# Down projection in chunks of 6 block pairs with portions of a plain chunk between them, operand sets split at set steps, gate2 rows loaded by halves

## The chip, the cores and the metric

The kernel runs on one core of one Trainium2 chip. The metric is the device time of one execution in microseconds. Before the change the median of three runs is 2086.94 us (2086.75 to 2090.03).

## What is computed

One layer of a decoder trunk on 512 tokens of width 2048, everything in fp32. The change touches its last part, the ConvGLU with its residual, and the computing of one of the six modulation vectors, gate2:

```python
mod = (c_act @ ada_w[l] + ada_b[l])[:, None, :]
shift1, scale1, gate1, shift2, scale2, gate2 = jnp.split(mod, N_MOD, axis=-1)
...
h = rms_norm(x, ffn_norm_g[l]) * (1.0 + scale2) + shift2
x = x + gate2 * conv_glu(h, w_up[l], conv_w[l], conv_b[l], w_down[l])
...
def conv_glu(h, w_up, conv_w, conv_b, w_down):
    a, v = jnp.split(h @ w_up, 2, axis=-1)
    ...
    for tap in range(CONV_WIDTH):
        conv = conv + conv_w[tap] * ap[:, tap:tap + S]
    return (jax.nn.silu(conv) * v) @ w_down
```

w_up is 2048 x 11264 and w_down 5632 x 2048. What lies ahead (the first norm, the input projection, a gated recurrence, a pooling branch and the output projection) isn't touched.

## The kernel before

**Products.** Activations stand with their features on the 128 partitions and the 512 tokens in the free dimension. Every fp32 operand is split into a high part in the matmul's number format (a cast on ScalarE, `L120` for weights, `L176` for activations) and a low part (a subtraction on VectorE, `L121` and `L177`). A product takes three matmuls: high by high, high by low, low by high.

**Up projection.** The 5632 features of the GLU are 44 blocks j of 128; a group makes the two 128 x 512 results (gate and value) of one j. The first three are computed plainly. The other 41 go through a scheme that makes a 2 x 2 block product from seven products instead of eight: with the tokens cut into halves of 256 and the two outputs and two halves of the input features as blocks. So a group is seven steps, one for each product, in the order `SEQ`, P1, Q5, P2, P7, Q3, P6, Q4. Each step runs over 8 pairs of feature blocks: 24 matmuls of 256 columns (`product`, matmuls at `L816` to `L818`). The operands on the token side (sums and differences of the halves of h) are split once and held in SBUF for all groups. Behind each group come the GLU of the group before (`glu`: two ScalarE operations `L722`, `L725`, four of VectorE, `L723` among them) and `emit`, which writes the results to DRAM: for the pairs of blocks that go through the seven products below as seven operands of 128 x 256 (`od`), for the last four blocks as they are (`ad`).

**Down projection.** It sums over the 44 blocks. Twenty pairs of blocks go through the same seven products in three chunks of `SD` = 7, 7 and 6 pairs; each chunk has eight groups, one for each pair of output blocks f and f + 8, and a step runs over the chunk's 7 or 6 pairs (21 or 18 matmuls of 256 columns). Behind a group its two results, times gate2, are added to x1, the residual (`L1120`); the 16 tiles of x1 come back from DRAM (`x1d`, `L1093`), two ahead of each group of the first chunk. The last four blocks (`JD`) are a plain product over the 16 output blocks, in two halves of 256 tokens, with the final norm behind each half.

**Weights.** Class `Fast` plans the weights of all groups by step number, seven to a group. `load` asks SyncE's queue for four tiles of 128 x (128 x pairs) a group, `first` adds two of them (`L773`, VectorE), `dsum` adds a third in place by an accumulating DMA on GpSimd's queue (`L779`), `fourth` is another sum (`L783`), and `split` makes the high and low part of each product's weights one or two steps ahead. Raw weights, gate2 rows and (before) operands on their way share 9 buffers of 128 x 1024 (`rp`); split weights have 3 (`wp`); everything of 128 x 512 shares 73 (`tp`).

**Operand sets.** A chunk's seven operand sets replace those of the stage before. Each engine works in the program's order, and the order is this: in the last group of a stage, right behind the product that used an old set, `handover` drops that set and calls `operands`, which loads the new set of the same product from `od` in two pieces of 3 or 4 pairs into `rp` (`L1056`) and splits it at once, two pairs an operation (`L176`, `L177`; a single pair at `L1065`, `L1066`). So every set is loaded and split within one group.

**gate2.** Each of its 16 tiles is a row pair of two 128 x 1024 halves, multiplied by the activation of c and summed along the row on VectorE (`L102`). In the groups 7, 9 to 37 the two halves are asked for behind P1 and multiplied behind Q4 (`ada_load`, `ada_tile`).

## Time and profile before

| what | before |
|---|---|
| median of three runs (range) | 2086.94 us (2086.75 to 2090.03) |
| profiled execution, its own time | 2086.09 us |
| span of its profile | 2084.3 us |
| mean granted TensorE clock | 0.993 |
| TensorE busy | 2016.5 us, 97% |
| VectorE busy | 1731.1 us, 83% |
| ScalarE busy | 1021.5 us, 49% |
| moved by DMA | 451.6 MB, 217 GB/s in the mean |

The shares are means over the whole span. The program is a row of stages, and each is read for itself: the groups of the up projection lie between about 960 and 1600 us, the three down chunks between 1600 and 2021, the final plain block and the norm behind that. A stretch is judged by the number of its matmuls and the time that they take when nothing is late.

### The profile page before, as it was taken

What the parts mean: (1) busy time and instruction counts of PE and PEld (TensorE: products, weight loads), DVE (VectorE), ACT (ScalarE), POOL (GpSimd) and SP (SyncE); (2) the same over time, 40 slices, a digit from 0 to 9 for tenths busy, and PEclk for the clock granted to TensorE, in tenths of its full rate; (3) what the DMA queues carried; (4) which work ended last, traced back from release to release, by engine and by line L of the source; (5) the groups of instructions that cost most, each with busy time, mean ns of one, the idle gap of its engine ahead of it and who ended that gap; (6) DMA issues with size and microseconds to landing.
All of it is one profiled execution on the core that took longest, in us unless ns stands there. A gap on an engine that the chain in (4) does not pass through costs nothing.

```text
span 2084.3 us, 36447 instructions
## 1 busy us (share of the span) xinstructions
PE 2016.5 (97%) x14450; PEld 1867.4 (90%) x14450; DVE 1731.1 (83%) x2668; ACT 1021.5 (49%) x1527; POOL 135.7 (7%) x171
## 2 busy tenths in 40 slices
PE   7999999999999998999999999999999998998997
PEld 6888888888888888999999999999999998998997
DVE  8898899988877689888888888888888868778786
ACT  4323555565733365545445445444546435445455
POOL 0100000000000000000000000000000100100101
PEclk9999999999999999999999999999999999999999
DMA  9886877755586545788887787887878868768662
GB/s 371 321 287 223 272 235 244 248 177 184 192 294 226 172 168 121 192 247 228 218 217 213 213 215 211 215 221 203 222 223 248 224 174 254 188 165 222 163 173 81
DMA packets 163466, 451.60 MB, mean 217 GB/s; under 512 B 15552, under 2 KB 55776, under 8 KB 163296
## 3 DMA queue, kind: packets, MB, share of 16 engines
q1 hardware_dynamic: 144576, 385.31, 55.0%
q0 software_dynamic: 18720, 63.97, 18.1%
q8 instruction: 113, 1.85, 0.4%
q14 instruction: 57, 0.47, 0.1%
HBM read 421.41 MB, written 27.80 MB: 216 GB/s over the span
## 4 chain that ended last, share of the span: by engine, by line
PE 60%; DMA 14%; DVE 14%; issue 8%; ACT 3%; POOL 0%; SPq 0%; DVEq 0%; ACTq 0%; POOLq 0%
DMA raw<-in_dram 13%; PE mm L149 8%; PE mm L151 7%; PE mm L150 7%; PE mm L818 6%; PE mm L816 6%; PE mm L817 6%; DVE w L121 5%; PE sm L816 4%; PE sm L817 4%; PE sm L818 4%; ACT w L120 2%; DVE raw L102 2%; DVE raw L773 2%; DVE raw L783 1%
## 5 line engine op out<-in xcount | busy, mean ns | idle before, releaser
L120 ACT CAST w<-raw 128x1024 fp32r<-128x1024 f32 (+2 forms) x579 | 579.5, 1009 | 633.7 <-DVE raw L783 189.6
L121 DVE TENSOR_TENSOR w<-raw,w 128x1024 fp32r<-128x1024 f32 (+2 forms) x579 | 674.4, 1171 | 194.2 <-ACT w L120 193.7
L818 PE MATMUL mm<-hh,w 128*128 128x256 f32 x1952 | 545.8, 280 | 19.0 <-DVE w L121 18.4
L816 PE MATMUL mm<-hh,w 128*128 128x256 f32 x1952 | 542.5, 278 | 4.6 <-ACT w L120 4.5
L817 PE MATMUL mm<-hl,w 128*128 128x256 f32 x1888 | 523.6, 277 | 0.7 <-DVE hl L177 0.7
L816 PE MATMUL sm<-hh,w 128*128 128x256 f32 x1464 | 407.7, 278 | 5.4 <-ACT w L120 4.9
L818 PE MATMUL sm<-hh,w 128*128 128x256 f32 x1464 | 407.9, 279 | 2.9 <-DVE w L121 2.7
L817 PE MATMUL sm<-hl,w 128*128 128x256 f32 x1416 | 394.3, 278 | 4.7 <-DVE hl L177 4.7
L818 PEld LDWEIGHTS mm<-hh,w 128*128 128x128 f32 x1952 | 367.7, 188 | 26.9 <-DVE w L121 26.6
L816 PEld LDWEIGHTS mm<-hh,w 128*128 128x128 f32 x1952 | 367.8, 188 | 6.2 <-ACT w L120 5.3
L817 PEld LDWEIGHTS mm<-hl,w 128*128 128x128 f32 x1888 | 355.6, 188 | 1.2 <-DVE hl L177 1.1
L149 PE MATMUL mm<-hh,w 128*128 128x512 f32 x800 | 313.7, 401 | 14.8 <-ACT w L120 12.9
L151 PE MATMUL mm<-hh,w 128*128 128x512 f32 x800 | 313.8, 392 | 0.0
L150 PE MATMUL mm<-hl,w 128*128 128x512 f32 x800 | 313.1, 392 | 0.0
L102 DVE SCALAR_TENSOR_TENSOR raw<-raw,ca 128x1024 f32<-128x1024 f32 x192 | 232.4, 1222 | 74.6 <-DMA raw<-in_dram 73.8
L816 PEld LDWEIGHTS sm<-hh,w 128*128 128x128 f32 x1464 | 277.0, 189 | 6.5 <-ACT w L120 5.5
L818 PEld LDWEIGHTS sm<-hh,w 128*128 128x128 f32 x1464 | 277.0, 189 | 4.7 <-DVE w L121 4.5
L817 PEld LDWEIGHTS sm<-hl,w 128*128 128x128 f32 x1416 | 268.1, 189 | 5.4 <-DVE hl L177 5.4
L779 POOL DMA_DIRECT2D raw<-in_dram x130 | 112.6, 866 | 1455.6 <-DVE raw L773 904.8
L149 PEld LDWEIGHTS mm<-hh,w 128*128 128x128 f32 x800 | 151.3, 189 | 46.3 <-ACT w L120 12.9
L151 PEld LDWEIGHTS mm<-hh,w 128*128 128x128 f32 x800 | 151.2, 189 | 33.1 <-DVE w L121 0.8
L150 PEld LDWEIGHTS mm<-hl,w 128*128 128x128 f32 x800 | 151.5, 189 | 30.4 <-issue 0.5
(207 smaller groups left out, 2302.9 us busy)
## 6 DMA issues: line engine op xcount, KB each, us to landing
raw<-in_dram SPq DMA_DIRECT2D x532, 512.0 KB, 5.0
raw<-in_dram POOLq DMA_DIRECT2D x82, 512.0 KB, 5.9
raw<-in_dram SPq DMA_DIRECT2D x64, 448.0 KB, 4.5
od<-t SPq DMA_DIRECT2D x60, 256.0 KB, 3.5
raw<-in_dram POOLq DMA_DIRECT2D x32, 448.0 KB, 6.8
raw<-in_dram SPq DMA_DIRECT2D x32, 384.0 KB, 4.1
raw<-od SPq DMA_DIRECT2D x21, 512.0 KB, 4.9
t<-in_dram SPq DMA_DIRECT2D x32, 256.0 KB, 6.1
```

Source lines behind the costliest of these rows:

```text
L102: V.scalar_tensor_tensor(out=r, in0=r, scalar=1.0, in1=vec[i], op0=ALU.mult, op1=ALU.mult, accum_out=a[:, i:i + 1])
L120: A.copy(h, r)
L121: V.tensor_tensor(l, r, h.bitcast(F32), op=ALU.subtract)
L149: E.matmul(o, wH, mH, start=start, stop=False)
L150: E.matmul(o, wH, mL, start=False, stop=False)
L151: E.matmul(o, wL, mH, start=False, stop=stop)
L773: V.tensor_tensor(r, self.raw[n, P1], self.raw[n, "T"], op=ALU.add)
L779: G.dma_start(self.raw[n, key], self.groups[n][q], accum_op=ALU.add)
L783: V.tensor_tensor(t, t, self.raw.pop((n, P2)), op=ALU.add)
L816: E.matmul(o, wH[:, sl], mH, start=first and k == 0, stop=False, skip_group_check=True)
L817: E.matmul(o, wH[:, sl], mL, start=False, stop=False, skip_group_check=True)
L818: E.matmul(o, wL[:, sl], mH, start=False, stop=k == len(opnd) - 1, skip_group_check=True)
```

## The change

- **Chunks.** `SD` becomes 6, 6 and 6 pairs: 18 pairs instead of 20. The four blocks that come free form a second plain chunk of four blocks (`JD` = 4 and 4). Its product over 16 output blocks is cut into 8 portions of two output blocks (`middle`): one raw weight tile, loaded four steps ahead and split two steps ahead, 24 matmuls of 512 columns, and two updates of x1. `MID` puts three portions ahead of the first chunk, three ahead of the second and two ahead of the third. Step numbers of `Fast` are moved by one for each portion.
- **Operand sets.** `operands` falls into `oload` (three loads of 256 KB into tiles of the 73-tile pool) and `osplit`, which `Fast` calls at set steps. With F the first step of a chunk and M = F - m the first step of its portions, the sets are split in the order of `SEQ` at M - 4, M - 2, M, M + 1, M + 2, F + 1 and F + 3, and loaded two steps before. `release` only drops the old sets (and, behind the last chunk, prepares the final plain block).
- **x1.** Six tiles are asked for ahead of the first portions, the other ten two at a time by the groups of the first chunk, as far as the portions have not.
- **gate2.** One half row is loaded behind P2 and multiplied behind P6 in each of the groups 7 to 38.

```diff
 NCH = T // P
 NJ = 44
 NP0 = 3
-SD = (7, 7, 6)
-JD = (4,)
+SD = (6, 6, 6)
+MID = (3, 3, 2)
+JD = (4, 4)
...
@@ -103,8 +104,8 @@
                                    accum_out=a[:, i:i + 1])
...
@@ -737,13 +738,21 @@
     class Fast:


-        def __init__(self, groups):
+        def __init__(self, groups, extra):
             self.groups = groups
             self.events = {}
             self.hl, self.raw = {}, {}
             self.at = -100
+            self.start = []
+            u = 0
             for n in range(len(groups)):
-                s = 7 * n
+                for _ in range(extra.get(n, 0)):
+                    s = 7 * n + u
+                    self.put(s - 4, partial(self.load_plain, u))
+                    self.put(s - 2, partial(self.split_plain, u))
+                    u += 1
+                s = 7 * n + u
+                self.start.append(s)
                 self.put(s - 7, partial(self.load, n, "T", 1))
                 self.put(s - 7, partial(self.load, n, P1, 0))
                 self.put(s - 4, partial(self.load, n, P2, 2))
@@ -765,6 +774,14 @@
             nc.sync.dma_start(r, self.groups[n][q])
             self.raw[n, key] = r

+        def load_plain(self, u):
+            r = rp.tile([P, U], F32, tag="raw", name="raw")
+            nc.sync.dma_start(r, w_dn[u])
+            self.raw["p", u] = r
+
+        def split_plain(self, u):
+            self.hl["p", u] = split_weights(self.raw.pop(("p", u)), U)
+
         def new(self, n):
             return rp.tile([P, U], F32, tag="raw", name="raw")[:, :self.groups[n][0].shape[-1]]

@@ -800,7 +817,8 @@
-    fast = Fast(groups)
+    NU = NJ - NP0
+    fast = Fast(groups, {NU + 8 * c: m for c, m in enumerate(MID)})
     nstep = [0]

     def product(n, i, opnd, banks):
@@ -957,12 +975,24 @@

     arow = {}

-    def ada_load(k):
-        arow[k] = gemv_load(ada[5 * KT + k])
-
-    for k in range(KT):
-        todo[7 + 2 * k, P1] = partial(ada_load, k)
-        todo[7 + 2 * k, Q4] = partial(ada_tile, 5, k, arow)
+    def ada_load(i):
+        arow[i] = r = rp.tile([P, U], F32, tag="raw", name="raw")
+        nc.sync.dma_start(r, ada[5 * KT + i // 2][:, i % 2 * U:(i % 2 + 1) * U])
+
+    def ada_half(i):
+        if i % 2 == 0:
+            arow["a"] = sp.tile([P, 2], F32, tag="acc", bufs=4, name="acc")
+        a, r, k = arow["a"], arow.pop(i), i // 2
+        V.scalar_tensor_tensor(out=r, in0=r, scalar=1.0, in1=ca[i % 2], op0=ALU.mult, op1=ALU.mult,
+                               accum_out=a[:, i % 2:i % 2 + 1])
+        if i % 2:
+            b = cs[:, C_AB + 5 * KT + k:C_AB + 5 * KT + k + 1]
+            V.scalar_tensor_tensor(out=mods[5][:, k:k + 1], in0=a[:, 0:1], scalar=a[:, 1:2], in1=b,
+                                   op0=ALU.add, op1=ALU.add)
+
+    for i in range(2 * KT):
+        todo[7 + i, P2] = partial(ada_load, i)
+        todo[7 + i, P6] = partial(ada_half, i)

     def group(n, opnds, ready=None, done=None):
         b = new_banks()
@@ -1029,6 +1059,7 @@
             return wH[:, c * P:(c + 1) * P], wL[:, c * P:(c + 1) * P]

     dn = Down()
+    dn.nl = NDS
     dact = []

     def act_pair(p):
@@ -1047,45 +1078,40 @@

     dop = []

-    def operands(c, i):
+    oraw = {}
+
+    def oload(c, i):
         p0, m = sum(SD[:c]), SD[c]
-        res = []
-        for q in range(0, m, 4):
-            w = min(4, m - q)
-            r = rp.tile([P, U], F32, tag="raw", name="raw")
-            nc.sync.dma_start(r[:, :w * 256].rearrange("p (m t) -> p m t", m=w),
-                              od[OIX[i], p0 + q:p0 + q + w].rearrange("m p t -> p m t"))
-            for g in range(0, w, 2):
-                src = r[:, g * 256:(g + min(2, w - g)) * 256]
...
-        return res
-
-    def handover(c, old):
-
+        oraw[c, i] = []
+        for q in range(p0, p0 + m, 2):
+            r = tt()
+            nc.sync.dma_start(r.rearrange("p (m t) -> p m t", m=2), od[OIX[i], q:q + 2].rearrange("m p t -> p m t"))
+            oraw[c, i].append(r)
+
+    def osplit(c, i):
+        dop[c][i] = []
+        for r in oraw.pop((c, i)):
+            dop[c][i] += split2(r)
+
+    for c, m in enumerate(MID):
+        F = fast.start[NU + 8 * c]
+        M = F - m
+        for i, t in zip(SEQ, (M - 4, M - 2, M, M + 1, M + 2, F + 1, F + 3)):
+            fast.put(t - 2, partial(oload, c, i))
+            fast.put(t, partial(osplit, c, i))
+
+    def release(old, c):
         def f(i):
             old[i] = None
-            if c < len(SD):
-                dop[c][i] = operands(c, i)
-            else:
-                act_more(min(JD[0] // 2, i))
+            if c == len(SD):
+                act_more(JD[0] // 2 + min(JD[1] // 2, i))
                 if i >= P6:
-                    if NDS:
-                        dn.load(2 * (i - P6) + 2)
-                        dn.split(i - P6 + 1)
-                    else:
-                        ws_next()
+                    ws_next()
         return f

     for m in SD:
         dop.append({})
-    x1 += [None] * KT
+    x1[:] = [None] * KT

     def x1_load(f):
         if f < KT:
@@ -1102,37 +1128,45 @@
             ws.extend(split(r[:, i * T:(i + 1) * T]) for i in range(2))

     pend = None
-    for n in range(NJ - NP0):
-        r = (n + NP0,) + group(n, hop, hop_ready if n == 0 else None, handover(0, hop) if n == NJ - NP0 - 1 else None)
+    for n in range(NU):
+        r = (n + NP0,) + group(n, hop, hop_ready if n == 0 else None, release(hop, 0) if n == NU - 1 else None)
         if pend is not None:
             emit(pend[0], glu(*pend))
         pend = r
     emit(pend[0], glu(*pend))
-    ng = NJ - NP0
+    act_more(JD[0] // 2)
+    ng, up = NU, 0
+
+    def middle(u):
+
+        fast.upto(nstep[0])
+        nstep[0] += 1
+        wH, wL = fast.hl.pop(("p", u))
+        for f in (2 * u, 2 * u + 1):
+            if x1[f] is None:
+                x1_load(f)
+            o = mm_ps() if f % 2 else sm_ps()
+            for k in range(JD[0]):
+                sl = slice((f % 2 * JD[0] + k) * P, (f % 2 * JD[0] + k + 1) * P)
+                mm3(o, wH[:, sl], wL[:, sl], *dact[k], k == 0, k == JD[0] - 1)
+            V.scalar_tensor_tensor(out=x1[f], in0=o, scalar=mods[5][:, f:f + 1], in1=x1[f], op0=ALU.mult, op1=ALU.add)
+
     for c in range(len(SD)):
+        if c == 0:
+            for f in range(2 * MID[0]):
+                x1_load(f)
+        for _ in range(MID[c]):
+            middle(up)
+            up += 1
         for f in range(8):
-            if c == 0:
-                x1_load(f)
-                x1_load(f + 8)
-            a, v = group(ng, dop[c], None, handover(c + 1, dop[c]) if f == 7 else None)
+            for i in (f, f + 8):
+                if x1[i] is None:
+                    x1_load(i)
+            a, v = group(ng, dop[c], None, release(dop[c], c + 1) if f == 7 else None)
             ng += 1
             for i, q in ((f + 8, v), (f, a)):
                 V.scalar_tensor_tensor(out=x1[i], in0=q, scalar=mods[5][:, i:i + 1], in1=x1[i], op0=ALU.mult, op1=ALU.add)
...
+    del dact[:JD[0]]
```

What this does to the queues shows at three places. Operations stand in the order in which their engine runs them, with the line, the result and operands, and the tile's shape; `x2` is two in a row.

VectorE, a group of the up projection with gate2's rows in it, before (`L102` is the multiplication of a half row, `L121` the low part of split weights, `L773` and `L783` the sums of raw weights, `L983` and `L985` the seven-product scheme's sums of results):

```order
L121 TENSOR_TENSOR w<-raw,w 128x1024
L726 TENSOR_TENSOR t<-t 128x512
L102 SCALAR_TENSOR_TENSOR raw,acc<-raw,ca 128x1024
L121 TENSOR_TENSOR w<-raw,w 128x1024 x2
L102 SCALAR_TENSOR_TENSOR raw,acc<-raw,ca 128x1024
L773 TENSOR_TENSOR raw<-raw 128x1024
L121 TENSOR_TENSOR w<-raw,w 128x1024
L983 TENSOR_TENSOR th<-th,mm 128x256
L783 TENSOR_TENSOR raw<-raw 128x1024
L111 SCALAR_TENSOR_TENSOR mod_102<-acc,cs 128x1
L121 TENSOR_TENSOR w<-raw,w 128x1024 x2
L985 TENSOR_TENSOR th<-th,sm 128x256
```

and after (`L986` is the half row, `L122` the low part of weights, `L790` and `L800` the sums):

```order
L122 TENSOR_TENSOR w<-raw,w 128x1024
L727 TENSOR_TENSOR t<-t 128x512
L986 SCALAR_TENSOR_TENSOR raw,acc<-raw,ca 128x1024
L122 TENSOR_TENSOR w<-raw,w 128x1024
L790 TENSOR_TENSOR raw<-raw 128x1024
L122 TENSOR_TENSOR w<-raw,w 128x1024 x2
L800 TENSOR_TENSOR raw<-raw 128x1024
L1013 TENSOR_TENSOR th<-th,mm 128x256
L122 TENSOR_TENSOR w<-raw,w 128x1024 x2
L1015 TENSOR_TENSOR th<-th,sm 128x256
```

Before, two half rows stand in one group, with two weight splits between them; after, one half row stands at the place of the first, and the next group has the other.

ScalarE, the change from the up projection to the first down chunk, before (`L120` weights, `L176` and `L1065` operands, `L722` and `L725` the GLU, `L977` to `L981` results copied from PSUM):

```order
L120 CAST w<-raw 128x1024 x4
L722 ACTIVATE t<-t,cs 128x512
L176 CAST hh<-raw 128x512
L120 CAST w<-raw 128x1024
L725 ACTIVATE t<-t 128x512
L977 COPY th<-mm 128x256
L176 CAST hh<-raw 128x512
L120 CAST w<-raw 128x1024
L176 CAST hh<-raw 128x512
L979 COPY th<-sm 128x256
L1065 CAST hh<-raw 128x256
L176 CAST hh<-raw 128x512
```

and after (`L121` weights, `L177` operands, whose source is `t` for the operand sets and `raw` for the plain chunk's activations, `L723` and `L726` the GLU):

```order
L121 CAST w<-raw 128x1024
L177 CAST hh<-t 128x512 x3
L121 CAST w<-raw 128x1024 x2
L177 CAST hh<-t 128x512
L121 CAST w<-raw 128x1024
L177 CAST hh<-t 128x512 x2
L121 CAST w<-raw 128x1024
L723 ACTIVATE t<-t,cs 128x512 x2
L177 CAST hh<-raw 128x512
L726 ACTIVATE t<-t 128x512
L177 CAST hh<-raw 128x512
L726 ACTIVATE t<-t 128x512
```

Before, one set of operands follows each product of the last up group. After, operand sets stand among the weights of the last up group and ahead of the last two GLU activations and of the plain chunk's operands, on which the first portion's matmuls depend.

SyncE's queue, the change from the first to the second chunk, before (`L765` weights, `L1056` operands, `L1093` x1):

```order
L765 DMA raw<-in_dram 128x896 x2
L1056 DMA raw<-od 128x4x256
L1056 DMA raw<-od 128x3x256
L1056 DMA raw<-od 128x4x256
L1093 DMA t<-x1d 128x512 x2
L1056 DMA raw<-od 128x3x256
L1056 DMA raw<-od 128x4x256
L1056 DMA raw<-od 128x3x256
L765 DMA raw<-in_dram 128x896
L1056 DMA raw<-od 128x4x256
L1056 DMA raw<-od 128x3x256
L1056 DMA raw<-od 128x4x256
```

and after (`L774` weights of the groups, `L779` weights of the portions, `L1088` operands, `L1119` x1):

```order
L1119 DMA t<-x1d 128x512 x2
L779 DMA raw<-in_dram 128x1024
L774 DMA raw<-in_dram 128x768 x2
L779 DMA raw<-in_dram 128x1024 x2
L1119 DMA t<-x1d 128x512 x2
L1088 DMA t<-od 128x2x256 x3
L774 DMA raw<-in_dram 128x768 x2
L1088 DMA t<-od 128x2x256 x3
L774 DMA raw<-in_dram 128x768 x3
L1088 DMA t<-od 128x2x256 x6
L774 DMA raw<-in_dram 128x768
```

Before, seven sets are asked for in pieces of 3 or 4 pairs within the last group; after, in pieces of two pairs, with the portions' and the next groups' weights between them.

## Rows read from the trace of the kernel before

**Rows 1.** Busy time of each engine over the span, page part 1 (share, instructions).

```profile
PE 2016.5 (97%) x14450; PEld 1867.4 (90%) x14450; DVE 1731.1 (83%) x2668; ACT 1021.5 (49%) x1527; POOL 135.7 (7%) x171
```

**Rows 2.** Stretches: length; busy PE, PEld, DVE, ACT, POOL (instructions); clock, DMA share, GB/s.

```profile
959.88:1600.46 640.58, 635.77 (x5570) 632.82 (x5569) 540.30 (x716) 318.22 (x414) 57.07 (x66) 1.00 0.81 217
1600.46:1646.58 46.12, 39.95 (x317) 38.24 (x316) 38.47 (x59) 23.84 (x39) 4.59 (x6) 0.96 0.92 262
1646.58:1745.04 98.46, 95.09 (x822) 93.69 (x820) 70.55 (x91) 43.34 (x62) 8.39 (x10) 1.00 0.73 195
1745.04:1797.71 52.67, 44.68 (x359) 42.74 (x358) 43.85 (x65) 28.37 (x47) 5.18 (x6) 0.97 0.80 225
1797.71:1893.05 95.34, 95.34 (x842) 95.29 (x841) 75.32 (x98) 47.37 (x68) 8.66 (x10) 1.00 0.71 181
1893.05:1934.04 40.99, 34.41 (x276) 33.02 (x274) 32.83 (x50) 20.22 (x33) 4.32 (x5) 0.96 0.83 223
1934.04:2021.38 87.34, 86.90 (x758) 86.17 (x757) 69.10 (x101) 43.29 (x67) 9.55 (x11) 1.00 0.72 186
```

**Rows 3.** Waits of VectorE, 930 to 1600 us: total, times, longest.

```profile
DVE raw L102 <- DMA raw<-in_dram: 21.4, 16, 1.9
```

**Rows 4.** VectorE in one up group: start, duration, operation, [idle before <-releaser].

```profile
1101.05 1.22 DVE L102 SCALAR_TENSOR_TENSOR raw<-raw,ca 128x1024 f32<-128x1024 f32 x1
...
1107.59 1.22 DVE L102 SCALAR_TENSOR_TENSOR raw<-raw,ca 128x1024 f32<-128x1024 f32 x1 [1.46 <-DMA raw<-in_dram]
...
1108.74 1.22 DVE L773 TENSOR_TENSOR raw<-raw 128x1024 f32<-128x1024 f32 x1
```

**Rows 5.** Two-microsecond stretches, TensorE alone: length, busy (matmuls), clock, DMA, GB/s.

```profile
1608.00:1610.00 2.00, 0.70 (x6) 1.00 1.08 237
...
1612.00:1614.00 2.00, 2.00 (x12) 0.52 0.99 363
```

**Rows 6.** VectorE by line and form, 1590-2025 us: busy, mean ns, idle before.

```profile
L177 DVE TENSOR_TENSOR hl<-raw,hh 128x512 fp32r<-128x512 f32 x67 | 45.9, 688 | 10.6 <-ACT hh L176 10.6
...
L1120 DVE SCALAR_TENSOR_TENSOR t<-t,mod 128x512 f32<-128x512 f32 x48 | 35.1, 748 | 0.3
...
L1066 DVE TENSOR_TENSOR hh<-raw,hh 128x256 fp32r<-128x256 f32 x13 | 5.5, 421 | 0.0
L121 DVE TENSOR_TENSOR w<-raw,w 128x1024 fp32r<-128x1024 f32 x3 | 3.7, 1221 | 0.3 <-DMA raw<-od 0.3
L723 DVE SCALAR_TENSOR_TENSOR t<-t,cs 128x511 f32<-128x511 f32 x2 | 1.4, 747 | 0.0
```

**Rows 7.** Time line of TensorE in a stretch of 512-column matmuls.

```profile
701.74 0.39 PE L150 MATMUL mm<-hl,w 128*128 128x512 f32 x1
...
703.78 0.39 PE L150 MATMUL mm<-hl,w 128*128 128x512 f32 x1
```

**Rows 8.** ScalarE by line and form, 1590-2025 us, columns as in 6.

```profile
L176 ACT CAST hh<-raw 128x512 fp32r<-128x512 f32 x68 | 39.9, 618 | 7.1 <-DMA raw<-od 7.1
...
L120 ACT CAST w<-raw 128x1024 fp32r<-128x1024 f32 x2 | 2.1, 1055 | 1.1 <-DVE raw L783 1.0
L722 ACT ACTIVATE t<-t,cs 128x512 f32<-128x512 f32 x2 | 1.5, 807 | 0.0
```

**Rows 9.** The 42 operand loads of line 1056: from issue to landing.

```profile
DMA to landing us min/median/max: 2.7/4.9/10.9
```

**Rows 10.** DMA issues, 1646.58-1745.04 us: count, size, median us to landing.

```profile
raw<-in_dram POOLq DMA_DIRECT2D x10, 448.0 KB, 7.3
t<-x1d SPq DMA_DIRECT2D x10, 256.0 KB, 7.3
```

**Rows 11.** DMA issues, 1797.71 to 1893.05 us.

```profile
raw<-in_dram POOLq DMA_DIRECT2D x10, 448.0 KB, 6.6
```

**Rows 12.** DMA issues, 1934.04 to 2021.38 us.

```profile
raw<-in_dram POOLq DMA_DIRECT2D x11, 384.0 KB, 5.9
```

More of the change, by code (lines that the diff above doesn't have):

```diff
@@ L104, in gemv, with ada_tile @@
         return a
-    def ada_tile(m, k, rows=None):
-        a = gemv(ada[m * KT + k], ca, rows and rows.pop(k))
+    def ada_tile(m, k):
+        a = gemv(ada[m * KT + k], ca)
         if (m, k) == (1, 0):
```

23 lines of the change are left out of this document (removed).

## The prediction

> **What bounds the kernel now.** The busy line of the page comes first: TensorE is busy for 97% of the span [rows 1]. That alone would leave little to win, so the next view is the same engine by stretches, with its matmuls counted [rows 2]. The reader should divide. The fifth stretch, the middle of chunk 2, runs 842 matmuls of 256 columns in 95.34 us, so one takes 113.2 ns when nothing is late. At that rate the other stretches should have taken less than they did: the up projection 630.5 instead of 640.6 us (10.1 lost); the change from up to down 35.9 instead of 46.1 (10.2); the rest of the first down chunk 93.1 instead of 98.5 (5.4); the change to the second chunk 40.6 instead of 52.7 (12.0); to the third 31.2 instead of 41.0 (9.7); the third chunk's rest 85.8 instead of 87.3 (1.5). The down blocks together lose 38.8 us. TensorE sets the end; what can be won is these waits.
>
> Next, who is late. In the up projection the waits of VectorE show one cause: 16 times, 21.4 us in all, it stands before a gate2 multiplication for its DMA [rows 3]. The time line shows what that pushes back: the first half of a row pair is multiplied without a wait, the second after 1.46 us, and the operations queued behind it (the sums and splits of the next weights) follow that much later [rows 4]. In the changes of chunk it is load. VectorE is busy 38.5 of 46.1 us and the DMA engines 92% of the first change, at 262 GB/s [rows 2]. There the clock also falls: after microseconds in which it ran only six matmuls in every two, the granted clock is 0.52, the 1.2 GHz level, and two microseconds hold 12 matmuls, where 113 ns would allow 17 or 18 [rows 5].
>
> A sum shows that VectorE's load explains the size. One splitting of an operand set of 7 pairs for all seven products is 21 splits of 0.688 and 7 short ones of 0.421 us, 17.4 us [rows 6]. A group of 7 pairs (7 x 7 x 3 matmuls, 16.6 us of TensorE) needs 75.32 x 16.6 / 95.34 = 13.2 us of VectorE, one of 6 pairs (14.3 us) 69.10 x 14.3 / 87.34 = 11.3, an up group (8 pairs, 19.0 us) 540.30 x 19.0 / 640.58 = 16.0, or 14.9 without gate2's 32 multiplications of 1.22 [rows 2, 4]. The second change thus holds 13.2 + 13.2 + 17.4 = 43.8 us of VectorE beside 33.3 of TensorE, 10.5 too many; 12.0 were lost. The third: 39.0 beside 30.9, 8.1 too many; 9.7 lost. The first (with 2.2 us for a second activation): 47.7 beside 35.7, 12.0 too many; 10.2 lost. The overload predicts each within 2 us.
>
> **Part by part. gate2.** 32 half rows, one a group instead of two in every second. The multiplications and bytes stay. Both halves now stand where the first stood, behind the third operation of an activation and ahead of one weight split. Its load was asked for in good time, since none of the 16 first halves waited [rows 3, 4]. VectorE reaches 16 us in each 19.0 us group, not 17 and 15. I let 9.5 of the 10.1 us go; bounds 0 and 10.
>
> **TensorE's own work.** Two pairs less: 2 x 8 groups x 7 products x 3 = 336 matmuls of 113.2 ns, 38.0 us. Four plain blocks more: 4 x 16 x 3 = 192 matmuls of 512 columns. Nine of these start in 2.04 us, 227 ns each [rows 7]: 43.6 us. So **+5.6 us**, certain.
>
> **First change.** The three plain portions (16.3 us of TensorE) stand between the last up group and the first down group. VectorE: 14.9 + 11.3 + 21 x 0.688 + three plain weight splits (3 x 1.22) + six x1 updates (6 x 0.75) + four splits of plain operands (2.8) + 2.2 = 53.9 beside 19.0 + 16.3 + 14.3 = 49.6, 4.3 too many [rows 2, 6]. But a wait of another kind is added. ScalarE's queue holds, ahead of the first plain operand, three operand splits that need their DMA, then a plain weight split that must wait for the last up product's buffer, and two convolutions. After the last up product that is 1.06 + 0.81 + 0.81 + 0.62 = 3.3 us, in which TensorE has nothing to run [rows 6, 8]. If these operand loads, issued behind a load that itself waits for a sum of VectorE, land after their median 4.9 us, they fit; at the longest, 10.9 us, they add about 5 [rows 9]. Five matmuls follow (1.1 us), and the low half stands behind two L723 and two L724 on VectorE (4 x 0.75), which costs about 2.7 more; the remaining low halves cost about 1. Seven us, then a slow clock as in [rows 5] (1.6) and a late tail (1.4): **10**, bounds 8 (the DMA bound below) and 16. So nothing is gained here.
>
> **Second change.** 11.3 + 11.3 + 14.5 + 3.7 + 4.5 = 45.3 of VectorE beside 14.3 + 16.3 + 14.3 = 44.9 of TensorE: 0.4 too many, and as before about 2 for order: **2.5**, bounds 1 and 12. **Third**, with two portions: 42.5 beside 39.4: 3.1 + 1.9 = **5**, bounds 2 and 10. The bytes allow it: two groups (12 weight loads of 384 KB), 21 operand loads of 256 KB, three plain weights and two x1 rows are 12.3 MB in 45 us, 273 GB/s; at 262 the engines were 92% busy, so 285 is full [rows 2]. In the first change the same count gives 16.5 MB, 58 us at 285 beside 49.6: at least 8 lost, if nothing is loaded earlier.
>
> **x1 loads.** Before, each group of the first chunk loads two tiles of x1; the accumulating loads then land after 7.3 instead of 6.6 us, and a group loses about 1 us (5.4 in 5.6 groups) [rows 2, 10, 11]. Now six tiles come ahead, ten in eight groups, and the weights are smaller (5.9 us landing in the last chunk [rows 12]): **2.5**, bounds 1 and 6. The other two chunks lose as the last one did, 1.5 in 6 groups: **3**, bounds 0 and 4.
>
> Sum: 10 + 2.5 + 5 + 2.5 + 3 = 23 instead of 38.8, a gain of 15.8; + 5.6; gate2 - 9.5. Net - 19.7 us. The profiled execution took 2086.09 (span 2084.3); the median of the three timed runs is 2086.94, so the time is about 2067. The final plain block and all ahead of the up groups keep their order.
>
> **Rivals.** *The portions cover everything*: as much VectorE work as TensorE's in the second change speaks for it, the first change's queue against. Losses 5 + 1 + 1 + 1 + 1 = 9: 38.8 - 9 - 5.6 + 9.5 = 33.7 less, 2053. *DMA takes VectorE's place*: 63 operand loads of 256 KB, 42 of up to 512 before, in stretches near 285 GB/s; in the crowded first chunk 256 KB took 7.3 us to land [rows 10]. If each change loses what it did, losses are 36: 2.8 - 5.6 + 9.5 = 6.7 less, 2080. The Trainium skill, "DMA: Bandwidth & Descriptors", section "Rules for kernel authors", speaks for this rival: it wants transfers joined, 1 MiB or more for full bandwidth; by its table our halved pieces would be less efficient. No row here compares one size with the other under equal load. *gate2's rows wait in every group*: half a row more often instead of whole rows; 32 waits of half the cost leave the 9.5 where they are, 2077. Against it stands that first halves never waited. *Slower*: SyncE issues in order, and operand loads into tiles of the 73-tile pool wait for TensorE to free them, with the next groups' weights behind. The pool has to hold 42 set tiles, 16 of x1, 8 plain operands, a group's results and three tiles for each set in flight. One product (2.04 us) lost per set load is 14 us a change, 42 in all on top of the 23: 38.8 - 65 - 5.6 + 9.5 is 22 more, 2109. It turns slower from 42.7 us of losses. Against it: in the new order these loads await products of a group already passed.
>
> **How the numbers follow.** Forecast 50%, everything covered 17%, DMA 16%, gate2 waits 9%, slower 6%, a mixture 2%. The range must leave out no more than the slower case and half of the best one: 2053 to 2080. Its bounds also take in a first change of 16, or one of 8 with the others at 1 and 2. 0.2% (4.2 us) is about what a measurement can tell from no change: below 2082.8 lie the first two cases, gate2 waits and most of the DMA case, 0.87; within, 0.07; above, 0.06.
>
> **What would show it.** The 16 waits of VectorE for gate2's DMA are gone and the up projection takes 631 us. Between the last up product and the first 512-column matmul TensorE stands for 3 to 4 us and the clock falls once. The second change shows gaps under 1 us each. Wrong would be: gaps there of 2 us or more ended by the DMA, or VectorE waiting for operand loads.

## The result, and the profile of the changed kernel

The changed kernel takes **2063.08 us** (three runs, 2062.34 to 2067.77) where the kernel before takes 2086.94: a ratio of **0.9887** (95% interval 0.9861 to 0.9914). Run again on another chip it gave 2065.74 us beside 2087.42, ratio 0.9892 (0.9872 to 0.9913). The forecast was 2067, its range 2053 to 2080. The profiled execution is the slowest of the three, 2067.77 us with a span of 2065.7, so two profiles differ by 18.3 us where the medians differ by 23.9. What follows is read between the two profiles; the other 5 us are spread between executions and no trace shows them.

The stretches answer to [rows 2]. The first begins with the same matmul as the first there; then come the first change with its three portions, six groups of the first chunk, the second change (the last group, three portions, the next group), six groups of the second chunk, the third change with two portions, and the rest. The columns are the same.

```profile
960.82:1592.45 631.63, 631.31 (x5570) 631.08 (x5568) 535.77 (x700) 316.67 (x401) 56.93 (x66) 1.00 0.83 218
1592.45:1632.25 39.80, 33.81 (x201) 29.53 (x199) 34.70 (x52) 23.31 (x39) 1.87 (x3) 0.91 0.89 274
1632.25:1725.04 92.79, 89.69 (x758) 87.14 (x757) 68.06 (x99) 39.59 (x60) 10.38 (x12) 1.00 0.67 173
1725.04:1773.70 48.66, 46.05 (x326) 42.45 (x325) 42.25 (x62) 27.61 (x44) 3.45 (x4) 1.00 0.85 250
1773.70:1859.89 86.19, 86.19 (x759) 85.96 (x757) 68.55 (x99) 40.01 (x60) 10.38 (x12) 1.00 0.69 168
1859.89:1902.69 42.80, 41.34 (x302) 38.23 (x301) 38.83 (x56) 25.70 (x42) 3.70 (x5) 1.00 0.90 263
1902.69:2002.95 100.26, 100.26 (x884) 100.21 (x883) 81.61 (x120) 50.58 (x79) 11.03 (x13) 1.00 0.73 184
```

Time lost is read as in the prediction: the length less 113.2 ns for each matmul of 256 columns and 227 ns for each of the 72, 72 and 48 of 512 columns in the changes. So the second row is 39.80 - 72 x 0.2267 - 129 x 0.1132 = 8.9.

| us lost in | before | predicted | measured |
|---|---|---|---|
| up projection | 10.1 | 0.6 | 1.1 |
| first change | 10.2 | 10 | 8.9 |
| first chunk, the rest | 5.4 | 2.5 | **7.0** |
| second change | 12.0 | 2.5 | 3.6 |
| third change | 9.7 | 5 | 3.2 |
| rest of the other chunks | 1.5 | 3 | 0.5 |
| down blocks in all | 38.8 | 23 | 23.2 |

The down blocks lose 15.6 us less and do 5.6 us more of matmuls; the up projection loses 9.0 less; 19.0 together, beside 18.6 between the spans. The sum was right, two of its terms were not, in opposite directions. The trace of the second measurement, read in the same rows, repeats them: 0.6, 9.7, 6.9, 3.0, 2.7 and 0.2 us lost, 22.5 in the down blocks.

**Up projection.** The waits of VectorE (930 to 1592 us: total, times, longest) have no row for gate2's multiplication any more. Below are the first three that the view gives; [rows 3] had 21.4 us there.

```profile
DVE w L122 <- ACT w L121: 83.4, 118, 3.8
DVE th L1015 <- PE sm L836: 11.4, 31, 0.4
DVE raw L790 <- DMA raw<-in_dram: 1.9, 1, 1.9
```

**First change.** TensorE's time line over the end of the last up product and the first portion (idle before, in brackets):

```profile
1592.33 0.28 PE L836 MATMUL mm<-hh,w 128*128 128x256 f32 x1
1597.36 0.50 PE L150 MATMUL sm<-hh,w 128*128 128x512 f32 x1 [4.75 <-ACT hh L177]
1597.69 0.48 PE L150 MATMUL mm<-hh,w 128*128 128x512 f32 x1
1597.98 0.63 PE L150 MATMUL sm<-hh,w 128*128 128x512 f32 x1
1598.40 0.63 PE L150 MATMUL mm<-hh,w 128*128 128x512 f32 x1
1598.83 0.63 PE L150 MATMUL sm<-hh,w 128*128 128x512 f32 x1
1600.70 0.79 PE L151 MATMUL sm<-hl,w 128*128 128x512 f32 x1 [1.25 <-DVE hl L178]
```

The engine stands until ScalarE has cast a plain operand, runs five matmuls, and stands again for the low half. Both stops were foretold. The first, 4.9 us from the end of one product to the start of the next, is 1.6 us longer than the 3.3 that the prediction put for the queue alone, and lies outside the 3 to 4 that it named as a sign. ScalarE's waits from 1583 to 1602 us say why: the operand sets' loads came late.

```profile
ACT hh L177 <- DMA t<-od: 2.7, 2, 2.4
```

Behind the stop the granted clock is at the 1.2 GHz level, and rises between 1604 and 1606 us, with TensorE busy again throughout from 1602 (columns as in [rows 5]):

```profile
1598.00:1600.00 2.00, 1.46 (x4) 0.50 0.96 268
1600.00:1602.00 2.00, 1.30 (x3) 0.50 0.98 328
1602.00:1604.00 2.00, 2.00 (x6) 0.50 1.06 387
1604.00:1606.00 2.00, 2.00 (x9) 0.83 1.04 409
```

**First chunk.** DMA issues from 1632.25 to 1725.04 us (count, size, median us to landing):

```profile
raw<-in_dram POOLq DMA_DIRECT2D x12, 384.0 KB, 6.4
t<-x1d SPq DMA_DIRECT2D x8, 256.0 KB, 5.9
```

and in the second chunk, from 1773.7 to 1859.9 us, where no x1 is loaded:

```profile
raw<-in_dram POOLq DMA_DIRECT2D x12, 384.0 KB, 5.6
```

The weights have the same size in both, VectorE's load is the same (68.06 and 68.55 us), and one chunk loses 7.0 and the other 0.3. The accumulating loads feed a weight that ScalarE casts next, and its waits for them are three times as long in the first chunk (the first row) as in the second:

```profile
ACT w L121 <- DMA raw<-in_dram: 10.3, 5, 2.5
...
ACT w L121 <- DMA raw<-in_dram: 3.2, 5, 0.8
```

**Second change.** The prediction's sign, gaps under 1 us and none ended by the DMA, came. This is the longest wait of TensorE from 1725.04 to 1773.70 us:

```profile
PE mm L836 <- DVE w L122: 0.9, 1, 0.9
```

Two questions were left: which part of the change earns the gain, and what the first change and the first chunk still wait for.

### The profile page after: what moved, and what is told of

It is laid out like the page before. It is cut to its first block, busy times and chain, and to the rows that moved or that the text cites. A ratio compares the mean times of both kernels' runs of the same rounds, so it can differ in the third digit from the quotient of the medians.

```text
span 2065.7 us, 36238 instructions
## 1 busy us (share of the span) xinstructions
PE 2013.6 (97%) x14306; PEld 1859.6 (90%) x14306; DVE 1730.8 (84%) x2674; ACT 1019.9 (49%) x1525; POOL 134.5 (7%) x171
## 4 chain that ended last, share of the span: by engine, by line
PE 78%; DVE 8%; DMA 6%; issue 5%; ACT 2%; POOL 0%; SPq 0%; DVEq 0%; POOLq 0%; ACTq 0%
PE mm L150 9%; PE mm L152 8%; PE mm L151 8%; PE mm L836 8%; PE mm L834 8%; PE mm L835 8%; PE sm L835 6%; PE sm L836 6%; PE sm L834 6%; DMA raw<-in_dram 6%; DVE w L122 2%; DVE raw L103 1%; PE sm L151 1%; PE sm L152 1%; PE sm L150 1%
## 5 line engine op out<-in xcount | busy, mean ns | idle before, releaser
L121 ACT CAST w<-raw 128x1024 fp32r<-128x1024 f32 (+1 forms) x587 | 578.0, 990 | 609.3 <-PE mm L152 158.9
L122 DVE TENSOR_TENSOR w<-raw,w 128x1024 fp32r<-128x1024 f32 (+1 forms) x587 | 670.7, 1146 | 200.6 <-ACT w L121 199.4
L836 PE MATMUL mm<-hh,w 128*128 128x256 f32 x1888 | 523.6, 277 | 6.3 <-DVE w L122 6.2
L834 PE MATMUL mm<-hh,w 128*128 128x256 f32 x1888 | 522.3, 277 | 0.7 <-ACT w L121 0.6
L836 PE MATMUL sm<-hh,w 128*128 128x256 f32 x1416 | 393.1, 278 | 1.8 <-DVE w L122 1.8
L834 PE MATMUL sm<-hh,w 128*128 128x256 f32 x1416 | 392.8, 277 | 0.8 <-ACT w L121 0.8
L836 PEld LDWEIGHTS mm<-hh,w 128*128 128x128 f32 x1888 | 354.4, 188 | 9.9 <-DVE w L122 9.6
L834 PEld LDWEIGHTS mm<-hh,w 128*128 128x128 f32 x1888 | 354.5, 188 | 2.1 <-ACT w L121 1.3
L150 PE MATMUL mm<-hh,w 128*128 128x512 f32 x832 | 325.3, 399 | 13.8 <-ACT w L121 12.8
L152 PE MATMUL mm<-hh,w 128*128 128x512 f32 x832 | 325.6, 392 | 0.0
L151 PE MATMUL mm<-hl,w 128*128 128x512 f32 x832 | 324.6, 391 | 0.3 <-DVE hl L178 0.3
L836 PEld LDWEIGHTS sm<-hh,w 128*128 128x128 f32 x1416 | 267.2, 189 | 3.1 <-DVE w L122 3.0
L834 PEld LDWEIGHTS sm<-hh,w 128*128 128x128 f32 x1416 | 267.0, 189 | 1.5 <-ACT w L121 1.0
L103 DVE SCALAR_TENSOR_TENSOR raw<-raw,ca 128x1024 f32<-128x1024 f32 x160 | 193.1, 1220 | 51.0 <-DMA raw<-in_dram 50.7
L150 PEld LDWEIGHTS mm<-hh,w 128*128 128x128 f32 x832 | 157.0, 189 | 46.3 <-ACT w L121 12.8
L152 PEld LDWEIGHTS mm<-hh,w 128*128 128x128 f32 x832 | 156.7, 188 | 34.3 <-DVE w L122 0.8
```

Of the source, the lines that this page charges most:

```text
L103: V.scalar_tensor_tensor(out=r, in0=r, scalar=1.0, in1=vec[i], op0=ALU.mult, op1=ALU.mult, accum_out=a[:, i:i + 1])
L121: A.copy(h, r)
L122: V.tensor_tensor(l, r, h.bitcast(F32), op=ALU.subtract)
L150: E.matmul(o, wH, mH, start=start, stop=False)
L151: E.matmul(o, wH, mL, start=False, stop=False)
L152: E.matmul(o, wL, mH, start=False, stop=stop)
```

## Experiments

For a whole kernel the down blocks are read as one stretch, from the end of the last up product to the start of the final plain block. So read, with the matmuls counted in the row, before loses 420.92 - 3362 x 0.1132 = 40.3 us and after 410.50 - 192 x 0.2267 - 3026 x 0.1132 = 24.4. The sums of the table are lower by 1.5 and 1.2, mostly because matmuls that run across the border of two stretches count in both. Before, then after:

```profile
1600.46:2021.38 420.92, 396.38 (x3362) 389.15 (x3361) 330.11 (x460) 206.43 (x314) 40.68 (x47) 0.99 0.76 204
...
1592.45:2002.95 410.50, 397.33 (x3218) 383.53 (x3217) 334.01 (x482) 206.80 (x323) 40.80 (x48) 0.99 0.76 203
```

Ratios are against the kernel before, timed beside each.

### gate2 by halves, alone

```diff
-    for k in range(KT):
-        todo[7 + 2 * k, P1] = partial(ada_load, k)
-        todo[7 + 2 * k, Q4] = partial(ada_tile, 5, k, arow)
...
+    for i in range(2 * KT):
+        todo[7 + i, P2] = partial(ada_load, i)
+        todo[7 + i, P6] = partial(ada_half, i)
```

> The kernel before with one edit: gate2's half rows, one a group, loaded behind P2 and multiplied behind P6. Theory: the 16 waits of VectorE for gate2's DMA are a cost of their own, paid in the up groups; the traces of before and after differ there by 8.6 us, so this kernel is 8 to 9 us faster than before, and its down blocks lose their 38 us as before. Rival 1: the waits end but the time comes back in the first change of chunk, which VectorE then reaches no earlier: 0 to 3 us faster. Rival 2: the up groups of after gained from something else (fewer tiles, other buffers): 0 to 2 us faster, and VectorE still waits for the rows.

2082.12 us beside 2087.90, ratio 0.9969 (0.9955 to 0.9983): 3.5 to 9.4 us faster. In its trace, the waits of VectorE in the up projection (930 to 1594 us), from the second row on:

```profile
DVE th L997 <- PE sm L818: 11.4, 31, 0.4
DVE raw L773 <- DMA raw<-in_dram: 3.6, 1, 3.6
```

and its down blocks:

```profile
1594.04:2017.65 423.61, 398.73 (x3362) 392.61 (x3361) 330.46 (x460) 206.70 (x314) 40.77 (x47) 0.98 0.76 203
```

The up products, from the first to the last, take 797.8 us instead of 806.1, 8.3 less. The down blocks lose 423.61 - 3362 x 0.1132 = 43.0 where before lost 40.3. The waits are a cost of their own, as the theory had it; but in this trace 2.7 of the 8.3 us went again in the down blocks, which the edit doesn't touch and which the theory had unchanged.

### Smaller chunks, alone

```diff
-SD = (7, 7, 6)
-JD = (4,)
+SD = (6, 6, 6)
+JD = (4, 4)
```

> The kernel before with only the sizes changed: three chunks of 6 pairs and two plain chunks of four blocks, both at the end, operand sets still loaded and split in the last group before their chunk. Theory (overload of VectorE): TensorE's own work grows by 5.6 us; a change between chunks holds 11.3 + 11.3 + 14.5 = 37.1 us of VectorE beside 28.5 of TensorE and loses about 9 to 10 us, as the third change of before does; the first change loses 10. In sum 0 to 3 us less waiting than before, so 2 to 6 us slower than before (2089 to 2093). Rival (a smaller set is what helps): 6 pairs fit, each change loses 3 us less or better, and the time falls by 4 us or more.

2100.85 us, ratio 1.0059 (1.0038 to 1.0080): slower, and by 7 us more than the upper end expected.

```profile
1604.09:1997.20 393.11, 365.35 (x3026) 353.99 (x3025) 305.48 (x445) 189.09 (x298) 40.77 (x47) 0.99 0.74 199
```

Lost are 393.11 - 3026 x 0.1132 = 50.6 us, ten more than before, and 6 us of matmuls come on top. The sum by VectorE's load (36 to 39) missed this: it counted the two groups of a change, and here the six groups behind each change also lose 5 to 15 us, which the sum had at 0 to 5. Why they don't recover was not followed up. The up projection, which the edit doesn't touch, also took 4.7 us longer in this trace, that of the slowest of five executions, so some of the 50.6 may be that execution's own; the medians are 13.0 us apart. That smaller sets alone help is refuted.

### Portions, with each set split in one group

```diff
-        for i, t in zip(SEQ, (M - 4, M - 2, M, M + 1, M + 2, F + 1, F + 3)):
-            fast.put(t - 2, partial(oload, c, i))
+        for i, t in zip(SEQ, range(M - 6, M + 1)):
+            fast.put(t, partial(oload, c, i))
             fast.put(t, partial(osplit, c, i))
```

> The kernel after, but each chunk's seven operand sets are loaded and split within the seven steps up to the first portion (steps M - 6 to M), each right behind the product that used the old set, as before the change. The portions stay. Theory: the portions give VectorE its time only if the splits are spread over them; put in one group they stand ahead of the portions' weight splits, and 11.3 + 14.5 = 25.8 us of VectorE fall beside 14.3 of TensorE: 6 to 9 us lost in the second and in the third change instead of 3.8 and 3.2, and as much or more in the first; 8 to 18 us slower than after (2071 to 2081). Rival: the portions alone do it, wherever the splits stand: within 3 us of after (2060 to 2066).

2084.24 us, ratio 0.9981 (0.9967 to 0.9995): nearly the whole gain is gone, 3 us above the top of what the theory gave.

```profile
1591.89:2021.42 429.53, 402.42 (x3226) 388.64 (x3225) 334.43 (x481) 207.49 (x321) 41.21 (x48) 0.97 0.72 193
```

Lost are 42.6 us (3034 matmuls of 256 columns, 192 of 512), 18 more than after. The second and third change lose 6.0 and 7.1, within the 6 to 9 expected. The first loses 18, far more than they do. There TensorE stands 16 us: with a set split right behind its load ScalarE's queue waits for the transfer. TensorE's time line there:

```profile
1608.86 0.80 PE L150 MATMUL sm<-hh,w 128*128 128x512 f32 x1 [15.87 <-ACT hh L177]
```

and ScalarE's waits from 1585 to 1612 us:

```profile
ACT hh L177 <- DMA t<-od: 9.5, 6, 3.3
```

So the two steps between a load and its use are part of what the set steps are worth. How much is theirs, and how much the spread over more steps, no run separates.

### Set steps, with the old sizes and no portions

```diff
-SD = (6, 6, 6)
-MID = (3, 3, 2)
-JD = (4, 4)
+SD = (7, 7, 6)
+MID = (0, 0, 0)
+JD = (4,)
...
```

> The kernel after with the sizes of before: chunks of 7, 7 and 6 pairs, no portions, one plain chunk at the end. Sets are split at the same steps as in after (F - 4 to F + 3), gate2 by halves. Theory: without portions the second change still holds 43.8 us of VectorE beside 33.3 of TensorE, so its loss of 12 stays within 3 us, and so do the others; against before only gate2's 8.6 and 0 to 6 us of the better spread are gained: 2073 to 2079. Rival: the spread over two groups is what the change lives by: each change loses 5 us or less and the time is 2064 or less, since this kernel also has 5.6 us less of matmuls than after.

2091.42 us, ratio 1.0021 (1.0007 to 1.0035): slower than before, though it has gate2's gain. Both theories are wrong. The down blocks, and then the first group of the second chunk:

```profile
1588.35:2024.21 435.86, 406.55 (x3365) 397.87 (x3364) 336.97 (x467) 213.72 (x324) 40.74 (x47) 0.96 0.73 198
...
1748.16:1780.38 32.22, 23.90 (x149) 21.76 (x148) 26.16 (x43) 18.62 (x34) 2.60 (x3) 0.84 0.91 264
```

54.9 us are lost, 15 more than before; this one group takes 32.2 us for 16.6 us of matmuls. Without portions M and F are the same step, and five of the seven sets fall due between F and F + 3. The DMA issues in that group:

```profile
t<-od SPq DMA_DIRECT2D x14, 256.0 KB, 7.0
...
raw<-in_dram POOLq DMA_DIRECT2D x3, 448.0 KB, 8.6
```

The operand loads land 7.0 us after issue instead of the 4.9 of [rows 9], the accumulating loads of the next weights 8.6, and VectorE is busy 26 of the 32 us. The steps were set for a change that is a portion block longer; without the block they bunch. As they are set here, only steps and portions together get below before's 40.3: portions alone lose 42.6 (8.0 less than small chunks without either), steps alone 54.9, both 24.4.

### x1 loaded at another place in the first chunk

```diff
-            for i in (f, f + 8):
-                if x1[i] is None:
-                    x1_load(i)
+            if c == 0 and f < 7:
+                todo[ng, P7] = partial(x1_two, f + 1)
+            if f == 0:
+                x1_two(f)
             a, v = group(ng, dop[c], None, release(dop[c], c + 1) if f == 7 else None)
```

> The kernel after with the x1 loads of the first chunk moved: a group asks for the next group's x1 tiles behind its fourth product (P7), not for its own at its start. Bytes and counts are the same. Theory: the 10.8 us that the first chunk of after loses behind its first group (7.1 in six groups, 3.7 in the seventh) come from x1 tiles loaded beside the accumulating loads, which land after 6.4 us there and after 5.6 in the second chunk, where the same groups lose 2.1. Moved out of that window, the chunk loses 2 to 4 us: 7 to 9 us faster than after. Rival: the lateness is left over from the first change, or the chunk's bytes are the cause wherever they stand: within 2 us of after, and the accumulating loads still land after 6.2 us or more.

2058.25 us (2057.22 to 2058.69) beside after's 2065.74 (2063.94 to 2066.97) on the same chip; ratio to before 0.9856 (0.9837 to 0.9876). Six groups of the first chunk:

```profile
1627.39:1715.95 88.56, 87.82 (x759) 86.77 (x757) 68.36 (x99) 39.82 (x60) 10.41 (x12) 1.00 0.74 188
```

their accumulating loads, and ScalarE's waits for them:

```profile
raw<-in_dram POOLq DMA_DIRECT2D x12, 384.0 KB, 5.9
...
ACT w L121 <- DMA raw<-in_dram: 5.5, 5, 1.6
```

The six groups lose 2.6 instead of 7.0 us, the group behind them 1.7 instead of 3.7. Same bytes, same count, another place: the accumulating loads land half a microsecond sooner, and ScalarE waits 5.5 us for them instead of 10.3. The theory holds: 7.5 us by the medians, within the 7 to 9 it gave, and 6.4 between the traces, a little below.

### The plain operands early

```diff
         def f(i):
             old[i] = None
+            if c == 0 and i in (P7, P6):
+                act_more(1 if i == P7 else 2)
...
-    act_more(JD[0] // 2)
```

> The kernel after with the plain chunk's four operands loaded and split inside the last up group (two behind its fourth, two behind its sixth product), not behind the last GLU. Theory: the 9.1 us lost between the last up product and the first down group (4.9 standing, then 4.2 of waits for low halves and a slow clock) are the queue of ScalarE ahead of these operands, not bytes or load: with the operands ready TensorE goes straight on, the granted clock stays at 1.00, and 5 to 9 us are gained. Rival (load): VectorE and DMA are full there (100% DMA share for 23 us), so the time comes back as waits of the portions or of the first down group: 0 to 3 us gained.

2063.06 us, ratio 0.9883 (0.9859 to 0.9907), beside 0.9892 for after: nothing gained that can be told. The portions, and the first group behind them:

```profile
1586.62:1603.48 16.86, 16.68 (x74) 13.45 (x73) 13.74 (x22) 8.54 (x13) 1.73 (x2) 1.00 1.01 300
1603.48:1625.25 21.77, 17.55 (x127) 16.36 (x126) 18.01 (x28) 11.15 (x19) 1.73 (x2) 0.92 0.88 267
```

TensorE doesn't stand at the portions any more: 72 matmuls in 16.86 us, where 16.3 is the least, and the clock stays up. Everything comes back one group later: 21.77 us for 126 matmuls, 7.5 lost where after lost 0.1. The queue of ScalarE was the last wait, not what bounds the change: the rival holds in the time, while which load it is, VectorE's or the DMA's, this run doesn't tell.

### Both

> The kernel after with both edits: x1 tiles asked for behind P7 for the next group, and the plain chunk's operands split inside the last up group. If both theories hold the gains add: 12 to 17 us faster than after. If VectorE or the DMA engines carry the lateness of the first change on into the first chunk, it gains less than the sum of the two alone by 4 us or more.

2057.24 us, ratio **0.9850** (0.9827 to 0.9872), the lowest ratio of the kernels timed, though it can't be told from the x1 edit alone (0.9856). Beside after on the same chip it is 8.5 us, where the x1 edit alone has 7.5 and the early operands 2.7. That is short of the 12 to 17 expected, but not by the 4 us below the sum that the other branch named: neither came. In the portions and the first group:

```profile
1589.67:1606.53 16.86, 16.68 (x75) 13.44 (x74) 13.66 (x21) 8.54 (x13) 1.73 (x2) 1.00 1.02 300
1606.53:1626.81 20.28, 15.95 (x127) 14.85 (x125) 18.10 (x28) 11.31 (x19) 1.72 (x2) 1.00 0.87 267
```

and VectorE's first wait from 1589 to 1630 us:

```profile
DVE t L1158 <- DMA t<-x1d: 2.6, 1, 2.6
```

The group still loses 6.0.

### The first x1 tiles inside the last up group

```diff
+            if c == 0 and i in (P2, P7, Q3, P6):
+                for k in (2 * i - 4, 2 * i - 3):
+                    if k < 2 * MID[0]:
+                        x1_load(k)
...
-        if c == 0:
-            for f in range(2 * MID[0]):
-                x1_load(f)
```

> The kernel of the two edits (x1 later in the first chunk, plain operands early) with a third: the six x1 tiles of the first portions are asked for inside the last up group, two behind each of P2, P7 and Q3, not behind it. In the kernel without this, VectorE stood 2.6 us for them between the portions, and the first down group lost 6.0 us. Theory (the order of the loads): with that wait gone 2 to 4 us of the 6.0 are regained, 2053 to 2055. Rival (VectorE has 53.9 us of work beside 49.6, and the DMA engines are full): the loss stays at 5 us or more, or moves into the portions or the first chunk; within 1.5 us.

2059.26 us, ratio 0.9854 (0.9825 to 0.9882). The wait for x1 is gone from VectorE, and the first down group loses 8.2 instead of 6.0. ScalarE's waits from 1586 to 1632 us show the new ones, for weights and operand sets whose loads stand behind the x1 tiles:

```profile
ACT w L121 <- DMA raw<-in_dram: 4.3, 1, 4.3
ACT hh L177 <- DMA t<-od: 3.6, 1, 3.6
```

The rival holds in the loss that stays; whether VectorE or the DMA engines make it is asked below.

### Portions 4, 2, 2

```diff
-MID = (3, 3, 2)
+MID = (4, 2, 2)
```

> As the kernel with x1 in the up group, but with portions 4, 2 and 2 instead of 3, 3 and 2. By the sum a portion covers 5.44 us of TensorE and itself costs VectorE 2.7, so it is worth up to 2.7 us where VectorE has more work than TensorE. Theory: the first change loses 2 to 3 us less, the second, which then has 42.6 us of VectorE beside 39.4 of TensorE as the third has, loses 1 us more than the 2.4 with three portions (the third loses 3.1 with two): in sum 0 to 2 us faster than with 3, 3, 2. Rival: the first change is bound by bytes, not by VectorE; a fourth portion brings it no more than 1 us and the second change loses 1 to 3 us more: 0 to 3 us slower.

2061.21 us, ratio 0.9866 (0.9839 to 0.9892), beside 0.9854 with 3, 3, 2: no difference that can be told. The trace follows the theory in the changes: the portions and the group behind them lose 5.5 instead of 8.7, the second change 4.0 instead of 3.3. And it gives it back in the six groups of the first chunk, which lose 7.5 instead of 3.5. In these traces a portion (and the two x1 tiles that come early with it) is worth some 3 us at the first change, and the chunk behind it takes them.

### Operand loads of 128 KB

```diff
-            nc.sync.dma_start(r.rearrange("p (m t) -> p m t", m=2), od[OIX[i], q:q + 2].rearrange("m p t -> p m t"))
+            for h in range(2):
+                nc.sync.dma_start(r[:, h * 256:(h + 1) * 256], od[OIX[i], q + h])
```

> The kernel after with each operand load of 256 KB cut into two of 128 KB: 126 loads in the place of 63, the same bytes, tiles and order. If the size of the pieces weighs in the changes of chunk, as a rule that wants large transfers says, loads land later and each change loses more: 5 to 15 us slower than after. My theory (VectorE's work and the order of the queues set the changes; the size was not what they waited for): 0 to 3 us slower, from 21 more issues a change of some 0.4 us each on SyncE's queue.

2068.59 us, ratio 0.9907 (0.9876 to 0.9939), beside 0.9892 (0.9872 to 0.9913) for after: 3 us by the ratios, within the intervals. The down blocks take 411.1 us instead of 410.5. Their landing, from 1725 to 1775 us:

```profile
t<-od SPq DMA_DIRECT2D x41, 128.0 KB, 4.7
```

The loads of 256 KB in after's second change:

```profile
t<-od SPq DMA_DIRECT2D x21, 256.0 KB, 5.2
```

Halving the pieces once more doesn't make the changes longer; pieces above 256 KB were not tried.

### Less work for VectorE in the first change

```diff
-            dop[c][i] += split2(r)
+            if c == 0:
+                h = tp.tile([P, T], F32R, tag="t", name="hh")
+                A.copy(h, r)
+                dop[c][i] += [(h[:, k * 256:(k + 1) * 256], h[:, k * 256:(k + 1) * 256]) for k in range(2)]
+            else:
+                dop[c][i] += split2(r)
```

> The kernel of the two edits (x1 later, plain operands early), leaving out one thing: the low halves of the first chunk's seven operand sets are not computed, the matmuls read the high halves in their place. TensorE, the transfers and the tiles loaded are the same; VectorE has 21 x 0.69 = 14.5 us less in the first change: 39.4 beside 49.6 of TensorE. Theory A (VectorE's load is what is left of the first change): the 6.0 us that its first down group lost fall to 1 or less, and the chunk behind it loses no more than its 5.4. Theory B (bytes: the DMA engines are full for some 20 us, and the accumulating loads of the first groups land late): 4 us or more stay in the first down group, ended by weights whose transfer comes late.

2056.28 us beside 2085.00, ratio 0.9872 (0.9849 to 0.9894): no gain over the kernel with both edits (0.9850). The portions and the first group:

```profile
1590.69:1607.40 16.71, 16.71 (x74) 13.37 (x73) 12.47 (x20) 9.46 (x15) 0.25 (x1) 1.00 1.04 341
1607.40:1628.95 21.55, 17.08 (x127) 16.28 (x126) 11.34 (x16) 10.91 (x18) 2.33 (x3) 0.92 0.84 235
```

VectorE is busy 11.3 us of the group's 21.6 instead of 18.1 of 20.3, and the group still loses 7.3. From 1590.69 to 1628.95 us the first wait of ScalarE:

```profile
ACT hh L1096 <- DMA t<-od: 9.2, 5, 2.7
```

of TensorE:

```profile
PE sm L834 <- ACT w L121: 3.5, 1, 3.5
```

and the DMA issues there:

```profile
t<-od SPq DMA_DIRECT2D x13, 256.0 KB, 7.2
...
raw<-in_dram POOLq DMA_DIRECT2D x3, 384.0 KB, 8.5
```

So VectorE's load is not what is left of the first change; only the seven groups behind lose less, 3.4 instead of 5.6. ScalarE stands 9.2 us for operand loads, which land 7.2 us after issue, and the weight cast that TensorE waits 3.5 us for stands in its queue behind casts of such late operands. Theory B had a weight's own transfer there. That transfers hold this stretch is shown for this kernel; whether by their bytes or by the order in which they are asked for stays open, since removing the splits also let the loads be issued closer together.

## Why the prediction held, and where it didn't

- **gate2: right.** 9.0 us of 10.1 went, 9.5 were foretold, and the 16 waits with them. Alone it was worth 5.8 us in the medians; in its trace the down blocks lost 2.7 more than before's.
- **TensorE's work: right.** The three portions of the second change take 16.35 us without a wait, 16.3 in the sum.
- **First change: right in size (8.9 for 10), wrong in what bounds it.** Both stops and the slow clock came, in other sizes (4.9 for 3.3, 1.3 for 2.7, and 2.5 to 3 us for 1.6); the late tail didn't come. But the working treats the queue of ScalarE as the cost. With the queue cleared the loss was still 8.0 (0.5 + 7.5). That meets the working's lower bound by bytes, "at least 8 lost", but doesn't confirm it. With the x1 edit as well the loss was 6.5 (0.5 + 6.0), below the bound. And 285 GB/s, which the bound takes for full, is no ceiling: two of the two-microsecond stretches above moved 387 and 409 GB/s, and [rows 5] already had 363. The overload of VectorE by 4.3 us, the other term there, isn't the bound either: with 14.5 us less of it the loss stays. What the last run shows is late operand loads with the weight casts behind them in ScalarE's queue; what makes the loads late stays open.
- **x1 loads: the term that was mis-sized.** 2.5 foretold, 7.0 measured, more than the 6 of its upper bound. The step that failed is the scaling by count: ten tiles in eight groups instead of sixteen, so less loss in proportion. The count isn't what sets the loss: the fourth to seventh group of before's chunk, with two tiles each, lose 1.0 to 1.8 us, the third to sixth of after's, with one, 0.7 to 1.9 (its first two lose nothing). What matters is the place. In after one tile is asked for between the group's two accumulating loads (in one group at 1662.57 us, the loads at 1661.83 and 1664.45), and that is enough to make these groups late. Moved 8 us ahead of them, the same tiles cost 4.4 us less.
- **Second and third change: 3.6 for 2.5, 3.2 for 5; right.** VectorE's sum put them far below the 12.0 and 9.7 of before, and they are. That VectorE's share is the reason is argued: no run took its work out of these two changes alone.
- **The rest of the chunks:** 0.5 for 3. Without x1 and without a late change ahead of it, a chunk loses nothing. This repaid a little more than half of what x1 was short by.
- **The sum.** That 23.2 meets 23 is in part luck: the first chunk lost 4.5 us more than its term and the second change 1.1 more, the other three terms together 5.4 less.
- **Rivals.** That the portions cover everything, with 9 us lost: not so, 23.2 are. That pieces of 256 KB would cost as much as VectorE did: with them 23.2 us were lost, not the rival's 36, and pieces of 128 KB cost nothing that can be told beside them; larger ones were not tried. By the rule of the Trainium skill ("DMA: Bandwidth & Descriptors", section "Rules for kernel authors": join transfers, 1 MiB or more) the halved pieces should have been less efficient; the runs show no loss beyond the intervals, and the down blocks of the traces differ by 0.6 us. That gate2's rows would wait in every group: not so. That SyncE's queue would block on tiles: not so, in the three changes the operand loads wait for TensorE's products 0, 1.0 and 1.1 us in all. The kernel without portions is slower than before, but not by this: in its second change they wait so for 0.3.
- **What the prediction did not see.** Portions without the steps, steps without portions, and small chunks without either lose 42 to 55 us in the down blocks, more than the 40 of before. The sum came out because it priced each change of chunk as it stands with all edits made; edit by edit it would have been wrong, and nothing in its text says that the edits hang on each other.

## What to carry to other kernels

Price a stretch by the work of each engine in it, and then ask what the DMA engines do in the same stretch: here, with the DMA engines full, clearing the last wait moved it to the next group. A load costs by when it runs, not only by its bytes; look for the transfer that lies on a chain (here the accumulating load ahead of a weight split) and keep others out of its few microseconds. Edits that share a schedule need measuring together as well as one by one: here each alone lost time in the down blocks.

## What was not expected of the hardware

- Operand loads cut to 128 KB landed after 4.7 us, those of 256 KB after 5.2, in the same change.
- After a stop of 4.75 us the granted clock was 0.50 in the three stretches of two microseconds from 1598 to 1604, the last of them full of matmuls, and 0.83 in the next; where the stop was avoided it stayed at 1.00 over the portions.
- Accumulating loads of 384 KB took 8.5 us to land in a change with DMA shares of 1.04 and 0.84, and 5.6 in the second chunk of after, at 0.69.
- A DMA share near 1 went with very different rates: two-microsecond stretches at 0.99 to 1.08 moved from 237 and 363 GB/s ([rows 5]) to 387 and 409 (in the first change of after).
